# Spreading cumulative sums by DMA, one PSUM tile for two products, and modulation products in fours, in a two-layer hybrid trunk

## The chip, the cores and the metric

One core of one Trainium2 chip runs the whole program in one launch. Its engines are TensorE (PE in the rows, with PEld for its weight loads), VectorE (DVE), ScalarE (ACT), GpSimd (POOL) and SyncE (SP, which here only issues DMAs). The metric is the device time in microseconds, the median of the runs.

## What is computed

Two layers of a trunk run for a prompt (one sequence of 512 tokens) and eight samples (4 new tokens each, 1024 tokens of past), 544 tokens in all, with a model width of 1024. Per layer:

```python
mod = silu(c) @ w_ada + b_ada                   # shift, scale, gate, twice
h   = RMSNorm(x) * (1 + sc1) + sh1
P   = h @ w_in                                  # one projection for all mixers
A   = sparse GQA attention (indexer, top 256)
B   = causal pooling with windows 2, 4, 8, 16
C   = Mamba-2 SSD scan, gated, group-normed
x  += g1 * (sum_b sigmoid(G_b) * (branch_b @ w_branch_b)) @ w_out
x  += g2 * ((silu(g) * a) @ ffn_down),  [a, g] = causal_dwconv3(h2 @ ffn_up)
```

The change lies in C and in `mod`. C has 32 heads of width 64 in 4 groups with a state of 128, and works in chunks of 128 tokens:

```python
cs       = cumsum(dt * A)                       # per head, within a chunk
Lmat     = where(causal, exp(cs_l - cs_s), 0)
y_diag   = (C.B^T * Lmat) @ (x * dt)
states   = B^T @ (x * dt * exp(cs_end - cs))
prev     = scan over chunks of (prev * exp(cs_end) + states)
y        = y_diag + (C @ prev) * exp(cs) + D * x
```

The conditioning vectors `c` are 9 (one prompt, eight samples); `w_ada` has 1024 x 6144 entries per layer.

## The kernel before, in words

Tokens lie along the free dimension (a tile is 128 x 544), channels on the partitions. Each big product (`gemm`, L325) streams one 128 x 1024 weight tile from HBM through SP into one of four buffers `raw`; ACT rounds it to `wh`, DVE makes the remainder `wl` (three buffers each), and PE does three passes per 128-row piece and half of the tokens (L336). Results go to one of two PSUM tiles `psg`.

Small work is written as generators and put between the GEMMs: each `gemm` calls `pump` (L136), which advances every lane by its rate in steps, where a step ends at a `yield`. Lane "c" carries the SSD's generators with 4 steps per GEMM during `ssd` (L863), lane "a" the modulation with 1. The program order so written is not the final one: the framework orders each engine's instructions ahead of the run by their place in the program and by when it reckons their inputs and buffers to be ready, and then each engine follows that fixed order. Weight loads (`high_priority`, also those of `ada`) count as 300 places earlier. All tiles made by `self.t` share slots by tag; the tag of `seg`, `ecs`, `csT`, `prev`, `h0` and most others has 49 slots, each 128 x 544 fp32. PSUM has three kinds of tiles with two buffers each: `psg` for GEMMs, and `psa` and `psb` for the small work.

`ada` (L235) computes `mod` for a third of its 6144 columns. For each of 4 column blocks it loads 4 tiles `raw` of 512 KB (L250) and does two products per tile (L253): `sc` (32 columns, 9 in use) is the stationary operand, 512 columns stream, and the result lands on a group of 32 PSUM partitions. Eight products make two rounds over the four groups, and the second round accumulates. A `yield` stands after each tile. The first third of layer 0 runs at the very start, the other two in `pool_branch` and attention, and those of layer 1 during the FFN of layer 0.

`dt_chain` (L619 and on) computes the cumulative sums, once with tokens on the partitions (`cs`) and once with heads on the partitions (`csT`, L693 to L698, rounded and with the remainder in rows 32 to 63).

`ssd` goes over 4 groups. In each there are 6 GEMMs with convolution and SiLU (B, C and four x tiles), 4 GEMMs for z, and 8 half-length GEMMs of the group before (`branch`). Each x tile (two heads) has a `ssd_chain` (L956): transposes (L965), the products with `dt` on DVE (L968) and with the decay on POOL (L970); then per head a product on PE that spreads a row of `csT` over 128 partitions (L978, with a 0/1 column of `selc` as the stationary operand), four subtractions on DVE that read it from PSUM (L982), two exponentials on ACT (L984, L985) and the product with `cb` on POOL (L986); then the chunk states (L992), the scan `prev` on DVE (L998), eight products with 64 result columns into a PSUM tile `y` (L1006), `Y` on DVE (L1010), and three products with `prev` into a second PSUM tile `yo` (L1015), which DVE multiplies by `ecs` (L1017) and POOL adds to `Y` (L1018). There are 16 chains per layer and 6 yields in each.

`ssd_sample` (L1028) does the samples once per group. Eight small products spread the samples' part of `csT` (L1049). In two halves of four samples, four state tiles `h0` of 256 KB are loaded through SP (L1084), and after a `yield` four products (L1088) write four groups of 32 partitions of `psa`; then per sample one product (L1100), an update on POOL (L1103) and DVE (L1106), and a store through ACT's queue (L1107).

The wait of an engine's instruction holds all that stands behind it on the same engine, DMA issues on SP, ACT and POOL included.

Of the kernel before, what the change touches and what calls it, by code (L numbers as in the profile page):

```python
# [35 lines left out]
T = SEQ + NS  # L36
# [67 lines left out]
class Prog:  # L104
# [90 lines left out]
    def consts(self):  # L195
# [15 lines left out]
        self.selc = self.cp.tile([128, 32], F32R, name="selc")  # L211
        nc.vector.tensor_copy(self.selc, c[:, C_SEL:C_SEL + 32])
# [22 lines left out]
    def ada(self, l, s, first=False):  # L235
# [8 lines left out]
        for c in range(4):  # L244
            ps = self.P("ada1")
            for z in range(4):
                i = 4 * c + z
                with self.tc.high_priority(offset=WPRI):
                    raw = self.wr.tile([128, 1024], F32, name="raw", tag="raw")
                    nc.sync.dma_start(raw, a["w_ada"][l, s, i])  # L250
                for q in range(2):
                    k, g = 2 * z + q, 32 * (2 * (z % 2) + q)
                    nc.tensor.matmul(ps[g:g + 32, :], self.sc[:, k, :], raw[:, q * 512:(q + 1) * 512],  # L253
                                     start=(k < 4), stop=(k >= 4))
                if z < 3:
                    yield
# [362 lines left out]
    def dt_chain(self, kd):  # L619
# [73 lines left out]
        ct = self.csT = self.t("csT")  # L693
        cr = ct.bitcast(F32R)
        nc.vector.memset(ct[64:128, :], 0.0)
        for so, do in ((o[:32, :], slice(0, 512)), (o2[:32, :32], slice(512, T))):
            self.copy("dt_chain20", cr[:32, do], so)
            self.E("dt_chain19").tensor_tensor(cr[32:64, do], so, ct[:32, do], op=OP.subtract)  # L698
# [257 lines left out]
    def ssd_chain(self, q, jj, xs):  # L956
        nc, a, l = self.nc, self.a, self.l
        par = self.par[l][0]
        csr = self.csT.bitcast(F32R)
        g, bt, cb, Cc = q["g"], q["bt"], q["cb"], q["C"]  # L960
        j = 4 * g + jj
        self.E("ssd_chain1").tensor_copy(q["xss"][:, jj, :], xs[:, 512:])
# [10 lines left out]
        mts = []  # L973
        ecs = self.t("ecs")
        for e in range(2):
            hd = 2 * j + e
            ps = self.P("ssd_chain2")
            nc.tensor.matmul(ps, self.selc[:, hd:hd + 1].to_broadcast([128, 128]), csr[:, :512], start=True, stop=True)  # L978
            d = self.t("seg")
            for i in range(4):  # L980
                s_ = slice(i * 128, (i + 1) * 128)
                self.E("ssd_chain4").tensor_scalar(d[:, s_], ps[:, s_], self.cs[:, i, hd:hd + 1], 0.0,  # L982
                                        op0=OP.subtract, op1=OP.min)
            nc.scalar.activation(ecs[64 * e:64 * e + 64, 128:512], ps[64 * e:64 * e + 64, 128:], AF.Exp)  # L984
            nc.scalar.activation(d[:, :512], d[:, :512], AF.Exp)  # L985
            self.E("ssd_chain5").tensor_tensor(d[:, :512], d[:, :512], cb[:, :512], op=OP.mult)  # L986
            mts.append(d)
            yield
# [12 lines left out]
        nc.gpsimd.dma_start(a["o_ssdp"][l, j], prev[:, 384:512])  # L1001
        yield
        y = self.P("ssd_chain4")
        for i in range(4):
            for e in range(2):
                nc.tensor.matmul(y[64 * e:64 * e + 64, i * 128:(i + 1) * 128],  # L1006
                                 xdt[:, i * 128 + 64 * e:i * 128 + 64 * e + 64],
                                 mts[e][:, i * 128:(i + 1) * 128], start=True, stop=True)
# [3 lines left out]
        yield  # L1012
        yo = self.P("ssd_chain5")
        for i in range(1, 4):
            nc.tensor.matmul(yo[:, i * 128:(i + 1) * 128], prev[:, (i - 1) * 128:i * 128],  # L1015
                             Cc[:, i * 128:(i + 1) * 128], start=True, stop=True)
        self.E("ssd_chain8").tensor_tensor(ecs[:, 128:512], ecs[:, 128:512], yo[:, 128:], op=OP.mult)  # L1017
        self.E("ssd_chain9").tensor_tensor(Y[:, 128:512], Y[:, 128:512], ecs[:, 128:512], op=OP.add)  # L1018
# [9 lines left out]
    def ssd_sample(self, q):  # L1028
        nc, a, l, c = self.nc, self.a, self.l, self.c
        par = self.par[l][0]  # L1030
        csr = self.csT.bitcast(F32R)
        g, cb, Cc, xss = q["g"], q["cb"], q["C"], q["xss"]
        ps = self.P("ssd_sample1")
# [13 lines left out]
        ps = self.P("ssd_sample2")  # L1047
        for i in range(8):
            nc.tensor.matmul(ps[:, i * 32:(i + 1) * 32], self.selc[:, 8 * g + i:8 * g + i + 1].to_broadcast([128, 128]),  # L1049
                             csr[:, 512:], start=True, stop=True)  # L1050
        ecs, mt = self.t("secs"), self.t("smt")
        for e in range(2):
            nc.scalar.activation(ecs[64 * e:64 * e + 64, :128].rearrange("p (j t) -> p j t", j=4),
                                 ps[64 * e:64 * e + 64, :256].rearrange("p (j e t) -> p e j t", e=2, t=32)[:, e],
                                 AF.Exp)
        m3 = mt[:32, :256].rearrange("p (h t) -> p h t", h=8)
        self.E("ssd_sample4").tensor_tensor(m3, ps[:32, :256].rearrange("p (h t) -> p h t", h=8),
# [17 lines left out]
        for hf in range(2):  # L1075
# [6 lines left out]
            h0s = [self.t("h0") for z in range(4)]  # L1082
            for z in range(4):
                nc.sync.dma_start(h0s[z][:, :512], a["h0"][l, g, 4 * hf + z])  # L1084
            yield
            for z in range(4):
                b = 4 * hf + z
                nc.tensor.matmul(qp[32 * z:32 * z + 32, :], cm[:, 32 * b:32 * b + 32], h0s[z][:, :512],  # L1088
# [680 lines left out]
```

## Time and profile before

| what | value |
|---|---|
| runs shown | 3218.22, 3217.64, 3216.38 us; median 3217.64 |
| profiled execution | 3219.4 us, span 3217.6 us, mean granted clock 0.985 |
| PE | 3117.6 us busy (97%), 24322 instructions |
| DVE | 2229.4 us (69%), 4827 |
| ACT | 1258.1 us (39%), 2228 |
| POOL | 892.9 us (28%), 1271 |
| DMA | 376.85 MB, mean 117 GB/s |

The span goes from the first to the last instruction. Busy time counts the time in which at least one instruction of an engine is under way; matmuls are pipelined, so several overlap. The two SSD stages lie at about 130 to 620 us (layer 0) and 1760 to 2260 us (layer 1). An fp32 product counts as two matmul instructions; those of L336, L978, L1049 and L1100 have rounded operands (fp32r) and count as one.

### The profile page before, as it was taken

What the parts mean: (1) busy time and instruction counts of PE and PEld (TensorE: products, weight loads), DVE (VectorE), ACT (ScalarE), POOL (GpSimd) and SP (SyncE); (2) the same over time, 40 slices, a digit from 0 to 9 for tenths busy, and PEclk for the clock granted to TensorE, in tenths of its full rate; (3) what the DMA queues carried; (4) which work ended last, traced back from release to release, by engine and by line L of the source; (5) the groups of instructions that cost most, each with busy time, mean ns of one, the idle gap of its engine ahead of it and who ended that gap; (6) DMA issues with size and microseconds to landing.
All of it is one profiled execution on the core that took longest, in us unless ns stands there. A gap on an engine that the chain in (4) does not pass through costs nothing. (4 is left out here: it accounts for less than half of the span.)

```text
span 3217.6 us, 63012 instructions
## 1 busy us (share of the span) xinstructions
PE 3117.6 (97%) x24322; PEld 2834.3 (88%) x24322; DVE 2229.4 (69%) x4827; ACT 1258.1 (39%) x2228; POOL 892.9 (28%) x1271
## 2 busy tenths in 40 slices
PE   7999999999999999999999999999999999999999
PEld 5987898999896788888989978989999967899999
DVE  5687788679878655444566877886799976564554
ACT  4344443333236534333443444433342365352432
POOL 2373445421021002111223544455120210030211
PEclk8999999999999999999999999999999999999999
DMA  6332332345433434445334323233233234333322
GB/s 231 104 104 77 110 95 101 105 151 179 164 117 129 157 133 115 147 146 147 105 104 122 98 82 106 89 96 119 95 129 117 91 125 154 106 84 94 78 98 78
DMA packets 303102, 376.85 MB, mean 117 GB/s; under 512 B 177362, under 2 KB 186930, under 8 KB 302802
## 3 DMA queue, kind: packets, MB, share of 16 engines
q1 hardware_dynamic: 116514, 315.94, 29.3%
q10 hardware_dynamic: 181216, 42.05, 6.4%
q0 software_dynamic: 5072, 14.83, 1.2%
q8 instruction: 192, 3.15, 0.4%
q14 instruction: 108, 0.88, 0.1%
HBM read 330.34 MB, written 33.79 MB: 113 GB/s over the span
## 5 line engine op out<-in xcount | busy, mean ns | idle before, releaser
L177 ACT ACTIVATE wh<-raw 128x1024 fp32r<-128x1024 f32 (+2 forms) x434 | 424.9, 980 | 1199.7 <-PE psg L336 909.6
L336 PE MATMUL psg<-hh,wh 128*128 128x272 f32 x4064 | 863.7, 292 | 7.8 <-ACT cacc L839 5.4
L336 PE MATMUL psg<-hl,wh 128*128 128x272 f32 x4064 | 856.0, 290 | 0.0
L336 PE MATMUL psg<-hh,wl 128*128 128x272 f32 x4064 | 853.6, 290 | 0.0
L322 DVE TENSOR_TENSOR wl<-raw,wh 128x1024 fp32r<-128x1024 f32 (+2 forms) x434 | 510.5, 1176 | 354.1 <-ACT wh L177 349.8
L336 PEld LDWEIGHTS psg<-hh,wh 128*128 128x128 f32 x4064 | 642.6, 189 | 61.9 <-issue 28.1
L336 PEld LDWEIGHTS psg<-hh,wl 128*128 128x128 f32 x4064 | 643.9, 189 | 17.1 <-issue 15.3
L336 PEld LDWEIGHTS psg<-hl,wh 128*128 128x128 f32 x4064 | 644.1, 189 | 15.9 <-issue 14.4
L841 POOL COPY sti<-cu 128x32 f32<-128x32 f32 x136 | 91.3, 672 | 588.9 <-ACT cu L177 588.6
L846 DVE SCALAR_TENSOR_TENSOR cacc<-cu,half,cacc 128x511 f32<-128x511 f32 x144 | 134.9, 937 | 6.8 <-ACT cacc L839 6.3
L336 PE MATMUL psg<-fh,wh 128*128 128x272 f32 x648 | 135.4, 291 | 2.6 <-DVE resid L460 2.6
L855 ACT ACTIVATE th<-cacc 128x544 f32<-128x544 f32 x92 | 60.5, 657 | 196.1 <-DVE cacc L849 187.5
L454 DVE SCALAR_TENSOR_TENSOR x<-psg,mod,x 128x272 f32<-128x272 f32 x64 | 32.0, 500 | 151.6 <-PE psg L336 142.6
L336 PE MATMUL psg<-fl,wh 128*128 128x272 f32 x648 | 133.7, 287 | 0.0
L336 PE MATMUL psg<-fh,wl 128*128 128x272 f32 x648 | 133.7, 288 | 0.0
L336 PEld LDWEIGHTS psg<-fh,wh 128*128 128x128 f32 x648 | 101.2, 188 | 14.3 <-issue 6.7
L336 PE MATMUL psg<-oh,wh 128*128 128x272 f32 x512 | 110.4, 294 | 0.0
L336 PE MATMUL psg<-ol,wh 128*128 128x272 f32 x512 | 109.5, 291 | 0.0
L336 PE MATMUL psg<-oh,wl 128*128 128x272 f32 x512 | 109.0, 292 | 0.0
L856 DVE SCALAR_TENSOR_TENSOR cacc<-th,cacc 128x544 f32<-128x544 f32 x92 | 71.3, 775 | 49.2 <-ACT th L855 49.0
L986 POOL TENSOR_TENSOR seg<-seg,cb 128x512 f32<-128x512 f32 x64 | 88.9, 1392 | 54.3 <-ACT seg L985 46.8
L336 PEld LDWEIGHTS psg<-fl,wh 128*128 128x128 f32 x648 | 101.7, 188 | 0.0
(469 smaller groups left out, 6232.4 us busy)
## 6 DMA issues: line engine op xcount, KB each, us to landing
raw<-wk SPq DMA_DIRECT2D x326, 512.0 KB, 3.5
raw<-w_ada SPq DMA_DIRECT2D x96, 512.0 KB, 3.5
h<-h SPq DMA_DIRECT2D x64, 256.0 KB, 3.8
raw<-wk SPq DMA_DIRECT2D x64, 256.0 KB, 2.8
o_ssds<-hn ACTq DMA_DIRECT2D x64, 256.0 KB, 2.2
raw<-wd SPq DMA_DIRECT2D x32, 448.0 KB, 3.4
kvr<-ckv SPq DMA_DIRECT2D x48, 256.0 KB, 3.6
kvw<-ckv SPq DMA_DIRECT2D x48, 256.0 KB, 4.0
```

What stands on the lines that cost most here:

```text
L177: self.nc.scalar.activation(out, src, AF.Copy)
L322: self.last_wl = self.E("weights1").tensor_tensor(wl[:, :n], raw[:, :n], wh[:, :n].bitcast(F32), op=OP.subtract).ins
L336: nc.tensor.matmul(o[:, c, :HC], w[:, k * 128:(k + 1) * 128], x[:, c * HC:(c + 1) * HC], start=(k == 0 and first), stop=(k == K - 1 and last))
L454: self.E("resid1").scalar_tensor_tensor(x[:, :HC], o[:, 0, :HC], g[:, 0:1], x[:, :HC], op0=OP.mult, op1=OP.add)
L841: self.E("conv1").tensor_copy(st[:, i, :, W - 1:], new)
L846: self.E("conv3").scalar_tensor_tensor(acc[:, s:512], u[:, :512 - s], wc, acc[:, s:512], op0=OP.mult, op1=OP.add)
L855: nc.scalar.activation(th, acc, AF.Tanh)
L856: self.E("silu21").scalar_tensor_tensor(acc, th, 1.0, acc, op0=OP.add, op1=OP.mult)
L986: self.E("ssd_chain5").tensor_tensor(d[:, :512], d[:, :512], cb[:, :512], op=OP.mult)
```

## The change

It has three parts. The cumulative sums with heads on the partitions are stored to DRAM once per layer (`csp`, `css`) and spread over the partitions by DMAs from ACT's queue: one row per head into a tile `seg` at the head of the chain, one row per group for the samples into `csb`. The chain's order changes: the states come ahead of the exponentials, the sums' exponential now has 128 partitions and multiplies C instead of the product with `prev`, and the products with `prev` (64 result columns each, two per chunk) add to the same PSUM tile as the diagonal ones; `yo`, `ssd_chain9` and three of the six yields go. In `ssd_sample` the `h0` loads of the first half stand at the head and those of the second right behind the first half's products, with one yield less per half. In `ada` two tiles are loaded before four products are issued; the number of yields stays.

```diff
-        self.selc = self.cp.tile([128, 32], F32R, name="selc")
-        nc.vector.tensor_copy(self.selc, c[:, C_SEL:C_SEL + 32])
...
@@ ada
-            for z in range(4):
-                i = 4 * c + z
-                with self.tc.high_priority(offset=WPRI):
-                    raw = self.wr.tile([128, 1024], F32, name="raw", tag="raw")
-                    nc.sync.dma_start(raw, a["w_ada"][l, s, i])
-                for q in range(2):
-                    k, g = 2 * z + q, 32 * (2 * (z % 2) + q)
-                    nc.tensor.matmul(ps[g:g + 32, :], self.sc[:, k, :], raw[:, q * 512:(q + 1) * 512],
-                                     start=(k < 4), stop=(k >= 4))
-                if z < 3:
+            for pair in range(2):
+                raws = []
+                for z in (2 * pair, 2 * pair + 1):
+                    with self.tc.high_priority(offset=WPRI):
+                        raw = self.wr.tile([128, 1024], F32, name="raw", tag="raw")
+                        nc.sync.dma_start(raw, a["w_ada"][l, s, 4 * c + z])
+                    raws.append(raw)
+                    if z % 2 == 0:
+                        yield
+
+                for k4 in range(4):
+                    nc.tensor.matmul(ps[32 * k4:32 * k4 + 32, :], self.sc[:, 4 * pair + k4, :],
+                                     raws[k4 // 2][:, (k4 % 2) * 512:(k4 % 2) * 512 + 512],
+                                     start=(pair == 0), stop=(pair == 1))
+                if pair == 0:
                     yield
@@ dt_chain
-        ct = self.csT = self.t("csT")
-        cr = ct.bitcast(F32R)
-        nc.vector.memset(ct[64:128, :], 0.0)
-        for so, do in ((o[:32, :], slice(0, 512)), (o2[:32, :32], slice(512, T))):
-            self.copy("dt_chain20", cr[:32, do], so)
-            self.E("dt_chain19").tensor_tensor(cr[32:64, do], so, ct[:32, do], op=OP.subtract)
+        ct = self.t("csT")
+        self.copy("dt_chain20", ct[:32, :512], o[:32, :])
+        self.copy("dt_chain20", ct[:32, 512:], o2[:32, :32])
+
+        self.csp = self.dp.tile([32, 512], F32, name="csp%d" % l)
+        self.css = self.dp.tile([4, 256], F32, name="css%d" % l)
+        nc.scalar.dma_start(self.csp, ct[:32, :512])
+        nc.scalar.dma_start(self.css.rearrange("g (h t) -> (g h) t", h=8), ct[:32, 512:])
@@ ssd_chain
+        segs = [self.t("seg") for e in range(2)]
+        for e in range(2):
+            nc.scalar.dma_start(segs[e][:, :512], self.csp[2 * j + e:2 * j + e + 1, :].to_broadcast([128, 512]))
...
-        mts = []
-        ecs = self.t("ecs")
-        for e in range(2):
-            hd = 2 * j + e
-            ps = self.P("ssd_chain2")
-            nc.tensor.matmul(ps, self.selc[:, hd:hd + 1].to_broadcast([128, 128]), csr[:, :512], start=True, stop=True)
-            d = self.t("seg")
-            for i in range(4):
-                s_ = slice(i * 128, (i + 1) * 128)
-                self.E("ssd_chain4").tensor_scalar(d[:, s_], ps[:, s_], self.cs[:, i, hd:hd + 1], 0.0,
-                                        op0=OP.subtract, op1=OP.min)
-            nc.scalar.activation(ecs[64 * e:64 * e + 64, 128:512], ps[64 * e:64 * e + 64, 128:], AF.Exp)
-            nc.scalar.activation(d[:, :512], d[:, :512], AF.Exp)
-            self.E("ssd_chain5").tensor_tensor(d[:, :512], d[:, :512], cb[:, :512], op=OP.mult)
-            mts.append(d)
-            yield
...
+        cds = []
+        for e in range(2):
+            hd = 2 * j + e
+            d, cd = segs[e], self.t("ecs")
+            nc.scalar.activation(cd[:, 128:512], d[:, 128:512], AF.Exp)
+            for i in range(4):
+                s_ = slice(i * 128, (i + 1) * 128)
+                self.E("ssd_chain4").tensor_scalar(d[:, s_], d[:, s_], self.cs[:, i, hd:hd + 1], 0.0,
+                                        op0=OP.subtract, op1=OP.min)
+            nc.scalar.activation(d[:, :512], d[:, :512], AF.Exp)
+            self.E("ssd_chain5").tensor_tensor(d[:, :512], d[:, :512], cb[:, :512], op=OP.mult)
+            self.E("ssd_chain8").tensor_tensor(cd[:, 128:512], cd[:, 128:512], Cc[:, 128:512], op=OP.mult)
+            cds.append(cd)
         yield
         y = self.P("ssd_chain4")
         for i in range(4):
+            s_ = slice(i * 128, (i + 1) * 128)
             for e in range(2):
-                nc.tensor.matmul(y[64 * e:64 * e + 64, i * 128:(i + 1) * 128],
-                                 xdt[:, i * 128 + 64 * e:i * 128 + 64 * e + 64],
-                                 mts[e][:, i * 128:(i + 1) * 128], start=True, stop=True)
+                nc.tensor.matmul(y[64 * e:64 * e + 64, s_], xdt[:, i * 128 + 64 * e:i * 128 + 64 * e + 64],
+                                 segs[e][:, s_], start=True, stop=(i == 0))
+            for e in range(2 if i else 0):
+                nc.tensor.matmul(y[64 * e:64 * e + 64, s_], prev[:, (i - 1) * 128 + 64 * e:(i - 1) * 128 + 64 * e + 64],
+                                 cds[e][:, s_], start=False, stop=True)
...
-        yo = self.P("ssd_chain5")
-        for i in range(1, 4):
-            nc.tensor.matmul(yo[:, i * 128:(i + 1) * 128], prev[:, (i - 1) * 128:i * 128],
-                             Cc[:, i * 128:(i + 1) * 128], start=True, stop=True)
-        self.E("ssd_chain8").tensor_tensor(ecs[:, 128:512], ecs[:, 128:512], yo[:, 128:], op=OP.mult)
-        self.E("ssd_chain9").tensor_tensor(Y[:, 128:512], Y[:, 128:512], ecs[:, 128:512], op=OP.add)
-        yield
@@ ssd_sample
+        def states(hf):
+            h0s = [self.t("h0") for z in range(4)]
+            for z in range(4):
+                nc.sync.dma_start(h0s[z][:, :512], a["h0"][l, g, 4 * hf + z])
+            return h0s
+        nxt = states(0)
+        csb = self.t("csb")
+        nc.scalar.dma_start(csb[:, :256], self.css[g:g + 1, :].to_broadcast([128, 256]))
...
-        ps = self.P("ssd_sample2")
-        for i in range(8):
-            nc.tensor.matmul(ps[:, i * 32:(i + 1) * 32], self.selc[:, 8 * g + i:8 * g + i + 1].to_broadcast([128, 128]),
-                             csr[:, 512:], start=True, stop=True)
...
-            h0s = [self.t("h0") for z in range(4)]
-            for z in range(4):
-                nc.sync.dma_start(h0s[z][:, :512], a["h0"][l, g, 4 * hf + z])
-            yield
+            h0s = nxt
             for z in range(4):
                 b = 4 * hf + z
                 nc.tensor.matmul(qp[32 * z:32 * z + 32, :], cm[:, 32 * b:32 * b + 32], h0s[z][:, :512],
                                  start=(hf == 0), stop=(hf == 1))
-            if hf:
+            if not hf:
+                nxt = states(1)
+            else:
```

In `ssd_sample` the two readers of the spread samples' sums (L1053 and L1057) read `csb` from SBUF instead of PSUM.

## Rows read from the trace of the kernel before

**Rows 1.** The page, part 4: the chain that ended last, by engine.
```profile
PE 33%; DVE 3%; issue 1%; DMA 1%; POOL 1%; ACT 1%; ACTq 0%; SPq 0%; DVEq 0%; POOLq 0%
```

**Rows 2.** Stages: from:to, length, busy PE PEld DVE ACT POOL, clock, DMA share, GB/s.
```profile
0.00:50.00 50.00, 32.00 (x156) 16.64 (x156) 25.57 (x84) 22.33 (x49) 11.82 (x39) 0.90 0.85 297
...
130.00:620.00 490.00, 477.65 (x3652) 430.12 (x3651) 381.24 (x718) 200.60 (x344) 248.33 (x284) 0.99 0.31 98
1760.00:2260.00 500.00, 488.16 (x3696) 436.88 (x3695) 385.95 (x722) 203.18 (x348) 251.16 (x284) 0.98 0.31 98
```

**Rows 3.** Timeline of PE near 1242 us: start us, us, instruction.
```profile
1241.64 0.42 PE L336 MATMUL psg<-hl,wh 128*128 128x272 f32 x2
1241.89 0.41 PE L336 MATMUL psg<-hh,wl 128*128 128x272 f32 x2
1242.23 1.05 PE L253 MATMUL psb<-raw,sc 128*32 128x512 f32 x4
1243.21 0.52 PE L336 MATMUL psg<-hh,wh 128*128 128x272 f32 x2
```

**Rows 4.** Timeline of PE near 718 us.
```profile
717.77 1.07 PE L253 MATMUL psb<-raw,sc 128*32 128x512 f32 x8
718.77 0.52 PE L1213 MATMUL psg<-ph,wh 128*128 128x272 f32 x2
```

**Rows 5.** Timeline of PE near 421 us and 200 us.
```profile
420.83 0.40 PE L978 MATMUL psa<-csT,selc 128*128 128x512 f32 x1
421.06 0.29 PE L336 MATMUL psg<-ol,wh 128*128 128x272 f32 x1
...
199.98 0.96 PE L1049 MATMUL psa<-csT,selc 128*128 128x32 f32 x8
200.79 0.49 PE L336 MATMUL psg<-hh,wl 128*128 128x272 f32 x2
```

**Rows 6.** Timeline of PE near 430 us.
```profile
428.26 0.43 PE L1006 MATMUL psb<-seg,xdt 128*64 128x128 f32 x2
428.63 0.39 PE L336 MATMUL psg<-oh,wl 128*128 128x272 f32 x1
...
431.12 1.09 PE L1006 MATMUL psb<-seg,xdt 128*64 128x128 f32 x14
432.14 0.94 PE L1015 MATMUL psb<-cacc,prev 128*128 128x128 f32 x6
432.83 0.50 PE L336 MATMUL psg<-oh,wh 128*128 128x272 f32 x2
```

**Rows 7.** Timeline of PE near 227 us.
```profile
226.31 1.04 PE L1088 MATMUL psa<-h,cm 128*32 128x512 f32 x2
227.29 0.52 PE L336 MATMUL psg<-hh,wh 128*128 128x272 f32 x2
```

**Rows 8.** DVE groups by shape: count, busy us, mean ns, idle before.
```profile
L982 DVE TENSOR_SCALAR seg<-psa,dtc 128x128 f32<-128x128 f32 x256 | 71.3, 341 | 11.4 <-PE psa L978 11.3
L1017 DVE TENSOR_TENSOR ecs<-ecs,psb 128x384 f32<-128x384 f32 x32 | 17.4, 545 | 2.2 <-PE psb L1015 2.2
L1381 DVE TENSOR_SCALAR S<-S,asm 128x128 f32<-128x128 f32 x32 | 8.7, 284 | 0.7
```

**Rows 9.** DVE groups by shape: L849, SSD (half) and FFN (fhalf).
```profile
L849 DVE SCALAR_TENSOR_TENSOR cacc<-sti,half,cacc 128x32 f32<-128x32 f32 x144 | 79.5, 552 | 3.0 <-POOL sti L841 2.2
L849 DVE SCALAR_TENSOR_TENSOR cacc<-sti,fhalf,cacc 128x32 f32<-128x32 f32 x88 | 21.3, 241 | 0.0
```

**Rows 10.** Timeline near 168 us: POOL, then DVE.
```profile
167.00 1.73 POOL L986 TENSOR_TENSOR seg<-seg,cb 128x512 f32<-128x512 f32 x1
...
167.51 1.28 DVE L849 SCALAR_TENSOR_TENSOR cacc<-sti,half,cacc 128x32 f32<-128x32 f32 x1
```

**Rows 11.** DMA issues (us to landing), and the issue itself (ns min/median/max).
```profile
h<-h SPq DMA_DIRECT2D x64, 256.0 KB, 3.8
...
L1107 ACTq DMA_DIRECT2D o_ssds<-hn x64: 338/339/555, 224.6 to 2259.0; - x64
```

More of the change, by code (lines that the diff above doesn't have):

```diff
@@ L958, in ssd_chain @@
         par = self.par[l][0]
-        csr = self.csT.bitcast(F32R)
         g, bt, cb, Cc = q["g"], q["bt"], q["cb"], q["C"]
         j = 4 * g + jj
+        segs = [self.t("seg") for e in range(2)]
+        for e in range(2):
+            nc.scalar.dma_start(segs[e][:, :512], self.csp[2 * j + e:2 * j + e + 1, :].to_broadcast([128, 512]))
         self.E("ssd_chain1").tensor_copy(q["xss"][:, jj, :], xs[:, 512:])
@@ L1030, in ssd_sample @@
         par = self.par[l][0]
-        csr = self.csT.bitcast(F32R)
         g, cb, Cc, xss = q["g"], q["cb"], q["C"], q["xss"]
+        def states(hf):
[6 more added lines that the diff above has]
+        nc.scalar.dma_start(csb[:, :256], self.css[g:g + 1, :].to_broadcast([128, 256]))
         ps = self.P("ssd_sample1")
@@ L1053, in ssd_sample @@
             nc.scalar.activation(ecs[64 * e:64 * e + 64, :128].rearrange("p (j t) -> p j t", j=4),
-                                 ps[64 * e:64 * e + 64, :256].rearrange("p (j e t) -> p e j t", e=2, t=32)[:, e],
+                                 csb[64 * e:64 * e + 64, :256].rearrange("p (j e t) -> p e j t", e=2, t=32)[:, e],
                                  AF.Exp)
         m3 = mt[:32, :256].rearrange("p (h t) -> p h t", h=8)
-        self.E("ssd_sample4").tensor_tensor(m3, ps[:32, :256].rearrange("p (h t) -> p h t", h=8),
+        self.E("ssd_sample4").tensor_tensor(m3, csb[:32, :256].rearrange("p (h t) -> p h t", h=8),
                                 self.cs[:32, 4, hs, None].to_broadcast([32, 8, 32]), op=OP.subtract)
```

## The prediction

> **What bounds the kernel now.** I read the page first: TensorE (PE) is busy 97% of the span, as the table above has it, and of the chain that ended last it holds 33 of the 40 points given [rows 1]. So I asked next how full each stage is. In the two SSD stages PE stands idle only 490.0 - 477.7 = 12.3 us and 11.8 us [rows 2]; VectorE (DVE) comes second with 77 to 78%, ScalarE (ACT) has 41%, GpSimd (POOL) 50%. The first 50 us are another case: DMA is 85% busy at 297 GB/s and DMA sets the pace [rows 2]. Elsewhere a microsecond of PE time that goes away is a microsecond of span, as long as DVE, ACT and POOL keep up. A busy sum does not give that time, since matmuls overlap; I take it from the timeline of PE, from the start of one piece to the start of the next. "Visit" means a run of instructions of one line between two pieces of the big GEMM (L336). These prices are at the full clock (granted 0.99 and 0.98 in the SSD stages [rows 2]).
>
> **A. Modulation products in fours (L253).** Each fp32 product is two instructions. A visit of two products (four instructions) lasts from 1242.23 to 1243.21, 0.98 us; two GEMM instructions take 1241.89 - 1241.64 = 0.25 us, so without the visit the next would have started at 1242.14, and entering costs 0.09 more: 1.07 us [rows 3]. A visit of eight instructions, where two pairs happened to meet, lasts 1.00 us, 1.09 with the entry [rows 4]: products that write different groups of 32 partitions run at the same time, four as cheaply as two. After the first 52 us there are 71 visits: 61 of four instructions, 7 of eight, three odd ones. The 61 become 30.5 of eight: 61 x 1.07 - 30.5 x 1.09 = 32 us, and the odd ones (20 instructions) give some 2 more: **34 us**. The 64 instructions of the first 50 us I set at nothing, because DMA hides them [rows 2]; holding two of the four weight buffers until a quad runs can cost some 3 us there. Later the weight stream keeps two buffers of four: at 297 GB/s [rows 2] a 512 KB tile takes some 2 us, and a GEMM of 48 instructions at 0.125 takes 6 us [rows 3].
>
> **B. The spreading products go.** A selection product (L978, 128x512) holds PE for 421.06 - 420.83 = 0.23 us, and there are 64: 14.7 us. Eight small ones of a group's samples (L1049) hold it 0.81 us, eight times: 6.5 us [rows 5]. Together **21 us**. The two PSUM tiles that they took are no longer asked for.
>
> **C. One PSUM tile per chain.** Now 28 of 32 chains send two instructions of L1006 alone (0.37 us), then fourteen (1.02 us), then six of L1015 (0.69 us) [rows 6]. After, six full-width instructions become twelve of half width. At 1.02/14 = 0.073 us they cost 0.87, or 0.18 more; one change of shape between the two lines, and its drain, goes. I take **0**. Bounds: 6 us lost (0.18 x 32) and 14 us won if the lone first pair is no longer sent ahead (0.37 + 0.09 each).
>
> **D. State loads earlier (L1084, L1088).** The four products of half a group also write four groups of 32 partitions, but 30 of their 40 visits hold one product only, and a visit of one costs as much as a visit of four: 226.31 to 227.29 is 0.98 us [rows 7], against 1.00 for eight instructions [rows 4]. With entries: 30 x 1.07 + 6 x 1.08 + 4 x 1.09 = 43 us, and 16 full visits would be 17. So up to 26 us lie here. The loads take 3.8 us to land [rows 11]; the change issues the first half's four pumped steps earlier and the second half's before the four updates instead of right ahead of the products. They need free slots of the shared pool of 49, which the longer lives of `seg`, `ecs` and `h0` make scarcer (only `csT` leaves). On SP they stand among the weight loads, which run two GEMMs ahead; a load that waits for a slot holds the weights behind it, covered for some 12 us. I take **14**, about half, because slots are scarce; bounds 0 and 26.
>
> **E. What is added.** ACT issues 64 loads of `seg`, 8 of `csb` and 4 stores, 76 DMAs. A 128-partition DMA holds ACT's queue 0.34 us [rows 11]: 26 us more on an engine at 41%. Behind each stand the copies of weights and of GEMM results; what is copied there is buffered two GEMMs deep, so a third of a microsecond is hidden; with no cover it would be the 26 us. The exponentials stay as many and as long in columns, so I count them as before. How long a row spread over 128 partitions takes to land no row shows: a 256 KB load needs 3.8 us [rows 11], and I take that, with anything from a third to three times of it as bounds, all of it behind the cover. The load starts at the head of a chain, and transposes, `xdd`, states and `prev` cover it; without that cover it would be 3.8 us for each of 32 chains. The subtraction waits anew for the first exponential, which reads the same tile; behind it on DVE stand weight remainders (L322), two GEMMs ahead of PE.
> The other addition is DVE's. The subtraction (L982) reads PSUM now, 256 x 0.341 us; a DVE operation of its size from SBUF (L1381) takes 0.284. The product on L1017 (0.545 us, one PSUM operand) is done twice per chain, both operands in SBUF [rows 8]. Against that stands what SBUF operands suffer beside POOL: the 128x32 step on L849 takes 0.241 us in the FFN, but 0.552 on average in the SSD stages [rows 9]. The timeline shows why: one that started at 167.51 ended at 168.79, just after POOL's multiply, which ended at 168.73 [rows 10]. With that mean wait of 0.31, DVE gets 256 x (0.284 + 0.31 - 0.341) = 65 and 64 x (0.545 + 0.31) - 32 x 0.545 = 37, some **102 us** more on 767 in 990, so 91% of a stage shortened to some 955. It stays below PE, but later results of DVE will stall it oftener. No row has that price. I bound it by 20 us of gain (today's 24 us of idle PE nearly gone, since fewer PSUM tiles are asked for) and 48 of loss (twice today's idling more), and take **12 us of new stalls**, half of today's idling again, because DVE stays below PE.
> [...]
>
> **The sum.** 34 + 21 + 0 + 14 - 12 = 57 us. The profiled execution took 3219.4 us with a span of 3217.6; the median of the runs, 3217.64, lies 1.8 below it. I take the 57 off the median: **3161 us**. A measurement tells about 0.2% here, 6.4 us.
>
> **The rivals.**
> *Everything fits (0.13):* all sixteen visits of D whole, no lone first pair, no new stall: 34 + 21 + 14 + 26 = 95, so 3123. For it: eight-instruction visits occur already. Against it: slots.
> *Late engines eat half (0.16):* ACT's issues and DVE's waits stall PE some 40 us: 3189. For it: DVE's 91%.
> *The quads come apart (0.08):* the second raw tile of a pair is late, the order sends two products ahead, and A gives nothing: 3195. Against it: weight loads are far ahead and 7 visits of eight formed by chance.
> *DVE becomes the bound (0.09), slower:* the place is the four subtractions and two products per head in the SSD stages, the price a wait w for POOL on each of 320 operations. DVE is then busy 767 + 3 + 320w. It decides once this passes 990 plus the 34 that A gives, at w = 0.79 us; the waiting operation of rows 10 waited 1.28 - 0.24 = 1.04. At w = 0.9 the stages take 1058, 68 more than now, less A: 3252. Against it: 0.31 is what L849 sees on average, and POOL loses the addition on L1018. [...]
> *The removed products were slack (0.02):* only if others hold the stages already, about 3217; rows 2 speak against it.
> The forecast keeps 0.52.
>
> **Range and chances.** 3115 to 3205 takes in the forecast with its bounds, most of the best case, the late engines and the split quads; the slower case stays out. Faster: 0.52 + 0.13 + 0.08 and nearly all of 0.16, 0.87. Within 0.2%: 0.04. Slower: 0.09.
>
> **What would show it.** A: visits of L253 with eight instructions, about 40 after the start, of 1.0 us. B: no selection products, no gaps in their place. C: one PSUM tile and a line with 28 instructions per chain. D: visits of the state products with eight instructions. E: the subtraction near 0.6 us on average with a long tail, DVE near 90% in the SSD stages and PE's idle time there some 35 us in all. I am wrong if DVE there passes 97%, if PE waits for `seg` or its loads, if quads stand as pairs, or if weight copies on ACT come late behind a DMA that waits for a slot.

## The result and the profile after

The changed kernel takes **3245.88 us** (median of 5 runs, 3240.77 to 3251.70) beside 3218.22 for the kernel before: ratio **1.0079**, 95% interval 1.0059 to 1.0099. It is slower by 0.8%, where I had forecast 3161 and a gain; it lies above the whole of my range. The profiled execution took 3240.77 us with a span of 3239.0 us and a mean granted clock of 0.971 (0.985 before).

The chain that ended last, part 4 of the page of the kernel after (answers to [rows 1]):

```profile
PE 29%; DVE 2%; issue 1%; ACT 1%; DMA 1%; POOL 0%; SPq 0%; ACTq 0%; POOLq 0%
```

No other engine has taken PE's place as the bound. The stages of the kernel after, columns as in [rows 2]:

```profile
130.00:620.00 490.00, 443.01 (x3470) 407.65 (x3469) 367.64 (x700) 187.84 (x324) 194.84 (x242) 0.94 0.34 108
1760.00:2260.00 500.00, 452.42 (x3554) 418.36 (x3554) 373.96 (x716) 193.92 (x334) 195.47 (x240) 0.95 0.34 107
```

PE stands idle 47.0 + 47.6 = 94.6 us there, 24.2 before, and its clock falls from 0.99 and 0.98 to 0.94 and 0.95. DVE, which I had feared, is at 75%, less than before. So PE waits, and nobody else is full: that is the picture of a **latency**, not of a busy engine. For what does it wait? The waits of PE in the kernel after, 130 to 620 us (engine, tile, line, releaser: us in total, times, longest):

```profile
PE psg L339 <- ACT cacc L844: 15.4, 2, 8.0
PE psb L1012 <- POOL seg L1004: 13.0, 6, 4.1
PE psb L1104 <- DVE hn L1110: 7.1, 3, 2.8
```

Before, the longest three of this list were 2.9, 2.6 and 1.4 us. The first two lines gave me two theories.

**Order.** PE's result products (L1012) wait for the masks that POOL finishes (L1004). The timeline of the kernel after, all engines, one chain of the second group (start us, us, instruction; in brackets the idle time of the engine before it and what ended it):

```profile
318.81 0.69 DVE L975 TENSOR_TENSOR xdt<-psa,dtc 128x512 f32<-128x512 f32 x1 [4.36 <-PE psb L1012]
...
319.58 1.05 POOL L977 TENSOR_TENSOR xdd<-xdt,dtc 128x512 f32<-128x512 f32 x1 [3.75 <-DVE xdt L975]
...
321.91 1.05 PE L983 MATMUL psb<-xdd,bt 128*128 128x128 f32 x8
...
323.00 0.28 ACT L177 ACTIVATE prev<-psb 128x128 f32<-128x128 f32 x1 [0.26 <-PE psb L983]
323.17 0.93 ACT L998 ACTIVATE ecs<-seg 128x384 f32<-128x384 f32 x2
...
323.93 0.47 DVE L989 SCALAR_TENSOR_TENSOR prev<-prev,dac,psb 128x64 f32<-128x64 f32 x2
...
324.31 0.68 DVE L1001 TENSOR_SCALAR seg<-seg,dtc 128x128 f32<-128x128 f32 x3
...
325.08 0.63 ACT L1003 ACTIVATE seg<-seg 128x512 f32<-128x512 f32 x1 [0.98 <-DVE seg L1001]
...
325.79 1.45 POOL L1004 TENSOR_TENSOR seg<-seg,cb 128x512 f32<-128x512 f32 x1 [5.16 <-ACT seg L1003]
...
327.30 0.47 PE L1012 MATMUL psb<-seg,xdt 128*64 128x128 f32 x1 [4.08 <-POOL seg L1004]
```

Read down the starts: `xdt`, `xdd`, the states on PE, and only then ACT's copy of the states, the exponentials, the subtractions, POOL's product, and PE again, 8.5 us after `xdt`, one link after another (two of the eight subtractions, at 320.07, had found a place earlier). Between the end of the states at 322.96 and 327.30 PE has only the rest of a GEMM, and stands idle 4.08 us.

**Queue.** The other line is the copy of a GEMM result on ACT. The timeline of ACT in the kernel after, with its queue:

```profile
206.03 7.18 ACTq L889 DMA_DIRECT2D sti<-st_conv  x4
213.25 1.30 ACTq L1041 DMA_DIRECT2D csb<-css  x1
214.60 0.81 ACT L844 ACTIVATE cacc<-psg,half 128x544 f32<-128x544 f32 x1 [8.83 <-DMA sti<-st_conv]
```

Small loads, which were there before, and the new `csb` load stand ahead of the copy for 8.8 us; four such places cost PE 31 us (8.0, 7.4, 9.5 and 6.5).

### The profile page after: what moved, and what is told of

Same layout as the page of the kernel before. It is cut to its first block, busy times and chain, and to the rows that moved or that the text cites. A ratio compares the mean times of both kernels' runs of the same rounds, so it can differ in the third digit from the quotient of the medians.

```text
span 3239.0 us, 63177 instructions
## 1 busy us (share of the span) xinstructions
PE 3062.8 (95%) x24386; PEld 2830.2 (87%) x24386; DVE 2236.2 (69%) x4852; ACT 1259.5 (39%) x2228; POOL 828.3 (26%) x1239
## 5 line engine op out<-in xcount | busy, mean ns | idle before, releaser
L846 POOL COPY sti<-cu 128x32 f32<-128x32 f32 x136 | 79.5, 584 | 555.5 <-ACT cu L177 555.5
L851 DVE SCALAR_TENSOR_TENSOR cacc<-cu,half,cacc 128x511 f32<-128x511 f32 x144 | 127.4, 885 | 16.9 <-ACT cacc L844 16.2
L1004 POOL TENSOR_TENSOR seg<-seg,cb 128x512 f32<-128x512 f32 x64 | 88.9, 1390 | 144.5 <-ACT seg L1003 144.3
L1001 DVE TENSOR_SCALAR seg<-seg,dtc 128x128 f32<-128x128 f32 x256 | 105.0, 447 | 13.1 <-DMA seg<-csp 12.8
L1578 POOL TENSOR_TENSOR cacc<-cacc 128x544 f32<-128x544 f32 x44 | 62.3, 1415 | 161.0 <-DVE cacc L861 161.0
```

The costliest lines, as they stand in the source:

```text
L846: self.E("conv1").tensor_copy(st[:, i, :, W - 1:], new)
L851: self.E("conv3").scalar_tensor_tensor(acc[:, s:512], u[:, :512 - s], wc, acc[:, s:512], op0=OP.mult, op1=OP.add)
L1001: self.E("ssd_chain4").tensor_scalar(d[:, s_], d[:, s_], self.cs[:, i, hd:hd + 1], 0.0, op0=OP.subtract, op1=OP.min)
L1578: self.E("ffn3").tensor_tensor(s_, s_, aa, op=OP.mult)
```

## The experiments

All times are medians beside runs of the kernel before on the same chip, with the 95% interval of the ratio. I name kernels by their labels. The runs come in sets, and the kernel before itself differs by up to 4 us from set to set (3218.12 to 3222.32), so a difference between kernels of two sets carries that much more doubt.

**1. One part alone: quads (e1), earlier state loads (e4).** e1 is the kernel before with only the `ada` part of the diff, e4 with only this (the first line at the head of `ssd_sample`):

```diff
+        nxt = states(0)
...
-            h0s = [self.t("h0") for z in range(4)]
-            for z in range(4):
-                nc.sync.dma_start(h0s[z][:, :512], a["h0"][l, g, 4 * hf + z])
-            yield
+            h0s = nxt
...
+            if not hf:
+                nxt = states(1)
```

> Before, with the modulation products in fours and nothing else. My prediction priced this part at 34 us, which would be 3184. The stages of the changed kernel in which these products run were 9 and 16 us shorter, so the theory that the SSD part alone makes the change slow expects about 25 us: 3190 to 3196, ratio 0.992. If the quads are what hurts elsewhere (a weight buffer held for longer), the gain is under 10 us.

> Before, with the state loads issued earlier and nothing else. My prediction priced this at 14 us of gain, bounds 0 and 26, so 3204 (3192 to 3218), seen as visits of the four state products in one piece. If the slots of the shared pool are the limit, the loads wait there, hold the weights behind them on SP, and the time rises by 5 us or more.

Measured: e1 3189.58, ratio 0.9906 (0.9891 to 0.9920), 30 us faster; e4 3210.11, ratio 0.9968 (0.9959 to 0.9978), 10 us faster. Both parts gain, so the loss is in the rest. In e4 the state products come in 20 visits instead of 40; its timeline of PE shows one that is whole and one that is not:

```profile
215.25 1.04 PE L1092 MATMUL psa<-h,cm 128*32 128x512 f32 x2
...
219.22 1.07 PE L1092 MATMUL psa<-h,cm 128*32 128x512 f32 x8
220.22 0.52 PE L336 MATMUL psg<-hh,wl 128*128 128x272 f32 x2
```

**2. The loads taken off ACT (e3).** The changed kernel with

```diff
-                nc.scalar.dma_start(st[:, i, :, 0:3], a["st_conv"][l, g, i])
+                nc.sync.dma_start(st[:, i, :, 0:3], a["st_conv"][l, g, i])
...
-        nc.scalar.dma_start(csb[:, :256], self.css[g:g + 1, :].to_broadcast([128, 256]))
+        nc.sync.dma_start(csb[:, :256], self.css[g:g + 1, :].to_broadcast([128, 256]))
```

> The changed kernel with the six small loads of a group's conv state and the spread of a group's sample sums issued from SP instead of ScalarE; the 64 spreads of the chains stay on ScalarE. Queue theory: the four waits of PE for the copy of a GEMM result, 31 us together, go: 3215 to 3222, ratio 0.992. Order theory: the waits for the masked matrix stay and the gain is under 10 us. If SP then holds the weights behind a load that waits for a slot, PE waits for weight loads, which the trace would show, and the time rises.

Measured: 3241.37, ratio 1.0067 (1.0054 to 1.0080): 4 us better than the change, and the intervals overlap. The waits of PE in e3, 130 to 620 us, tell why:

```profile
PE psb L1012 <- POOL seg L1004: 13.2, 6, 3.9
PE psb L750 <- ACT rel L748: 8.6, 2, 6.9
PE psg L339 <- ACT cacc L844: 6.4, 2, 4.7
```

The wait for the copy shrank from 15.4 to 6.4, and a wait for a relu, a little later on the same engine, grew from 3.1 to 8.6; PE's idle time in the two stages is 92.6 us instead of 94.6. **The queue theory falls as the main cause.** The largest single wait in a list need not be what the time hangs on: as these rows read, PE had no other work at that spot, so the next late engine held it instead.

**3. The steps of a chain restored (e2), and both edits (e6).** e2 is the changed kernel with three yields put back, nothing else:

```diff
         nc.gpsimd.dma_start(a["o_ssdp"][l, j], prev[:, 384:512])
+        yield
...
             cds.append(cd)
-        yield
+            yield
...
                                        op0=OP.mult, op1=OP.add)
+        yield
         yield
```

With four steps per GEMM, three steps put a whole chain between two GEMMs; with six, the result products fall behind the next one.

> The changed kernel with the steps of a chain cut as they were (six steps for each chain instead of three, so that the states and the result products fall into different GEMMs again); no operation is added or removed. Order theory (the chain's exponentials, subtractions and POOL multiply lie bare because states and result products now stand between the same two GEMMs): PE's waits for the masked matrix, some 27 us in the two SSD stages, mostly go, and the time falls by 20 to 35 us, to 3210 to 3225. Queue theory (DMA issues on ScalarE stand ahead of the copies of GEMM results): the 31 us of waits for that copy stay, and the time falls by less than 10. Theory of VectorE's waits for GpSimd: no change within 5 us.

> The changed kernel with both edits: the steps of a chain cut as before, and the small loads of a group issued from SP. With the chain's steps back (3212) PE still waited four times, 28.6 us in all, for the copy of a GEMM result behind these loads on ScalarE. Queue theory: those waits go now that the order gives other work, 3185 to 3192. If the stall only turns into the next one, as it did when the loads were moved alone (a wait for the result of a relu, then the conv chain): above 3203.

Measured: e2 3211.77, ratio 0.9971 (0.9958 to 0.9984), 34 us off; e6 3203.10, ratio 0.9948 (0.9929 to 0.9968), some 8 more, with intervals that overlap. The waits of PE in e2, 130 to 620 us:

```profile
PE psg L339 <- ACT cacc L844: 14.0, 2, 8.0
PE psb L1013 <- POOL seg L1005: 6.1, 5, 2.5
```

The wait for the masks is down from 13.0 to 6.1 us, and the one for the copy is nearly as it was. So the order of the work counts, but e2 is still some 30 us above what quads and earlier loads alone would make, though it has no selection products any more.

**4. The remaining parts one by one (e5, e7, e8).** e5 is quads and earlier loads. e7 adds to it the single PSUM tile alone: PE still spreads `csT`, `ecs` gets 128 partitions per head and is multiplied by C, both products go into `y`. e8 adds to e5 the spreading by DMA alone, with two PSUM tiles. In both the masks stay ahead of the states, with six steps. The core of e8:

```diff
-            ps = self.P("ssd_chain2")
-            nc.tensor.matmul(ps, self.selc[:, hd:hd + 1].to_broadcast([128, 128]), csr[:, :512], start=True, stop=True)
-            d = self.t("seg")
+            d = segs[e]
+            nc.scalar.activation(ecs[64 * e:64 * e + 64, 128:512], d[64 * e:64 * e + 64, 128:512], AF.Exp)
...
```

> Before, with the quads (alone 30 us faster) and the earlier state loads (alone 10 us faster), nothing else. If the two add: 3180, ratio 0.987. If the loads of the quads' second weight buffer and the earlier state loads hold each other up on SP: nearer to 3190.

> Quads and earlier state loads (some 3180), and of the rest only the one PSUM tile: both products of a chain add into it, the decay is multiplied onto the second operand for each head on VectorE (one product more for each chain), while TensorE still spreads the cumulative sums, and the chain keeps six steps in the old order. My prediction set this part at 0 (bounds 6 lost, 14 won): 3166 to 3186. If the single tile is what hurts (nothing of the second product can run until the result products of the first have their masks, and the product on VectorE comes ahead of PE's line): 3195 or more.

> Quads and earlier state loads (some 3180), and of the rest only the spreading by DMA: the selection products go, ScalarE issues the loads of each chain and group, the subtraction reads SBUF; the chain keeps its six steps in the old order and its two products stand apart in two PSUM tiles. If the spreading itself is sound, as my prediction had it (21 us off, at most 12 of stalls): 3160 to 3172. If the DMA issues on ScalarE, the landing of the loads, or the subtraction beside GpSimd is what loses time whatever the order: 3185 or more, with waits of PE for a copy on ScalarE or for the masked matrix.

Measured: e5 3183.10 (0.9888, 0.9870 to 0.9905); e7 3173.46 (0.9850, 0.9832 to 0.9869), 10 less than e5; e8 3153.48 (0.9784, 0.9764 to 0.9804), 30 less than e5 and below the 3160 to 3172 I expected. With the old order each of the four parts pays. What is left as a suspect is the new order.

**5. Order, crossed with the number of steps (e9, e10), and the loads again (e11).** e9 is the whole change with the block of exponentials, subtractions and mask products put back ahead of the states, in six steps; e10 the same in three; e11 is e9 with the edit of e3.

```diff
+        cds = []
+        for e in range(2):
...
         stp = self.P("ssd_chain3")
...
         nc.gpsimd.dma_start(a["o_ssdp"][l, j], prev[:, 384:512])
-
-        cds = []
-        for e in range(2):
...
         yield
         y = self.P("ssd_chain4")
```

> The whole change, but the chain in the old order: spread, subtraction, exponentials and mask product ahead of the states, and six steps for each chain. The parts alone gave: quads and earlier loads 3183, with the single PSUM tile 10 less, with the DMA spreading 30 less. Order theory: only the order loses, so the parts add to 3183 - 10 - 30 = 3143, 3138 to 3152. If single tile and DMA spreading hurt each other (the products on VectorE now both from SBUF, beside GpSimd): 3165 or more.

> The whole change with the exponentials ahead of the states again, but the chain still in three steps, so that masks, states and result products fall between the same two GEMMs. The six steps with the exponentials behind gave 34 us. If number of steps and place cost independently: some 34 above the six-step kernel of this set, about 3177. If the place alone does the harm: within 10 us of that kernel. If the steps do most of it: above 3190.

> The whole change in the old order with six steps, and the small loads of a group (conv state, sample sums) issued from SP. If the loads on ScalarE still hold copies of GEMM results there: 5 to 15 us under the kernel without this edit. If the old order covers them, as it covered them before the change: within 5 us of it.

Measured (ratio, us):

| masks | six steps | three steps |
|---|---|---|
| ahead of the states | e9 3142.94, 0.9761 (0.9746 to 0.9775) | e10 3164.02, 0.9817 (0.9797 to 0.9838) |
| behind the states | e2 3211.77, 0.9971 (0.9958 to 0.9984) | the change 3245.88, 1.0079 (1.0059 to 1.0099) |

As times the parts add to within 1 us (3143 forecast); by the ratios it is some 5 us, since the two sets' kernels before differ by 4. The place costs 3211.77 - 3142.94 = 69 us with six steps, the steps 21 us with the masks ahead and 3245.88 - 3211.77 = 34 with the masks behind, both together 103. So place and steps don't cost independently: e10 lies between the two cases I had named for it (3177, and within 10 us of e9). e9 is also the version that **beats both kernels**, by 79 us against before. e11 takes 3149.90 (0.9781, 0.9764 to 0.9797), 7 us more than e9 with overlapping intervals: with the old order nothing is gained by taking the small loads off ACT. That PE's other work covers the burst there, as before the change, fits this and the waits below.

The stages and the waits of PE in e9, 130 to 620 us (columns of the stages as in [rows 2]):

```profile
130.00:620.00 490.00, 473.74 (x3836) 436.48 (x3835) 405.68 (x776) 206.35 (x356) 229.66 (x271) 0.99 0.39 120
1760.00:2260.00 500.00, 483.41 (x3880) 448.60 (x3880) 408.24 (x786) 202.55 (x354) 219.08 (x261) 0.98 0.39 119
```

```profile
PE psa L972 <- DVE cb L958: 6.0, 1, 6.0
PE psb L1105 <- DVE hn L1111: 4.4, 3, 1.7
PE psb L1012 <- POOL seg L990: 2.3, 2, 1.9
```

Idle time of PE is 16.3 + 16.6 = 32.9 us, the clock is back at 0.99 and 0.98, the wait for the masks is down from 13.0 to 2.3, and that for the copy from 15.4 to 1.4, though nothing was done about it. In e10, where only the steps are missing, the wait for the masks is back:

```profile
PE psb L1011 <- POOL seg L990: 9.2, 6, 6.0
```

**6. The order alone, in the kernel before (e12).** Before, with the selection products, subtractions, exponentials and mask products moved as a block behind the states, six steps, nothing added.

> Before, with one thing moved: in each chain the spreading, the subtraction, the exponentials and the mask product stand behind the states, as in the changed kernel; six steps, two products apart, spreading by TensorE, nothing added or removed. Order theory: the place alone loses time, 20 to 60 us, so 3238 to 3280, with waits of PE for the masked matrix. If the place hurts only together with the DMA spreading or the single tile: within 6 us of before.

Measured: 3298.90, ratio 1.0245 (1.0229 to 1.0261): 77 us slower, more than the 20 to 60 expected. The place needs neither the DMAs nor the single tile to do its harm. The stages of e12:

```profile
130.00:620.00 490.00, 455.09 (x3372) 408.80 (x3371) 353.86 (x680) 190.22 (x324) 213.63 (x251) 0.95 0.29 89
1760.00:2260.00 500.00, 464.27 (x3461) 418.77 (x3462) 361.39 (x691) 190.71 (x322) 216.32 (x258) 0.96 0.31 92
```

One of my signs failed, though: PE's waits put down to the masks are only 1.6 us in either stage there, and the copies of GEMM results (13 us in each) lead the list. A list of waits names where a lateness comes out, which need not be where it starts.

**7. What in the place does it (e13, e14).** e13 is e2 with the states' matmuls left ahead, but their evacuation moved behind the mask products:

```diff
-        prev = self.t("prev")
-        self.copy("ssd_chain10", prev[:, :128], stp[:, :128])
...
-        nc.gpsimd.dma_start(a["o_ssdp"][l, j], prev[:, 384:512])
         yield
...
             cds.append(cd)
-            yield
+            if e == 0:
+                yield
+        prev = self.t("prev")
+        self.copy("ssd_chain10", prev[:, :128], stp[:, :128])
...
+        nc.gpsimd.dma_start(a["o_ssdp"][l, j], prev[:, 384:512])
+        yield
```

e14 is e2 with the copy of the first state on DVE (`CPD` gets `ssd_chain10`).

> The whole change with six steps and the states' matmuls ahead of the masks, as changed, but the evacuation of the states (the copy on ScalarE, the six steps of the scan on VectorE, the store) moved behind the mask products. The kernel with evacuation ahead took 3212, the one with everything in the old order 3143. Queue theory of the place (the copy and the scan wait for the states' product, and the exponentials and subtractions stand behind them on the same two engines, though their own loads have landed): 3143 to 3160, and the time from the states' product to the second mask falls from 6.9 to some 3.6 us. If the place of the matmuls on TensorE is what counts: 3200 or more.

> The kernel with six steps and the masks behind the states (3212), with only the copy of the first state moved from ScalarE to VectorE. If ScalarE's queue is what holds the exponentials (it waited 31 us in each SSD stage for the states in this kernel): 3175 to 3195. If the scan on VectorE ahead of the subtractions does it alone or as well: within 10 us of 3212.

Measured: e13 **3153.01**, ratio 0.9791 (0.9775 to 0.9807), 59 of the 69 us regained; e14 3207.98, ratio 0.9959 (0.9946 to 0.9973), within 4 us of e2. The tile `prev` in the kernel after, 130 to 620 us (the engine that works on it sat idle before it, us and times, until):

```profile
  PE psb L983: 33.9, 12
  ACT prev L177: 15.1, 6
```

and in e13:

```profile
  DVE prev L1006: 22.4, 12
  PE psb L983: 5.5, 5
```

ACT's copy waited 33.9 us for the states and DVE's scan 15.1 us for that copy, with the exponentials and the subtractions behind them in the same two queues, although their loads had landed: a load of `seg` takes 3.6 us in the median, and DVE waited 12.8 us for one in the whole program, 15 times in 256 subtractions. With the evacuation behind the masks, the wait for the states is 5.5 us (8.1 in e9, 5.8 before); the 22.4 are POOL's wait ahead of the store, which is 24.5 in e9 and so not what costs. From the trace, the time from the end of the states' last product to the end of the second mask product is, in the median of 32 chains:

| evacuation ahead of the masks | us | masks ahead of it | us |
|---|---|---|---|
| the change | 6.9 | before | 3.0 |
| e2 | 6.9 | e9 | 3.6 |
| e14 | 6.9 | e10 | 3.8 |
| e12 | 6.5 | e13 | 3.9 |

Some 3.3 us more per chain, times 32, is 106 us of latency, of which 69 come out. The number of steps leaves this latency as it is (e2 beside the change, e10 beside e9); what it alters is how long PE has to wait for the masks. e14 shows that it isn't ACT alone: with the copy on DVE the latency is still 6.9, so the scan is as much in the way of the subtractions. The 10 us between e13 and e9, and which of the three yields matters, the runs do not separate.

## Why the prediction was wrong

**Where the time went.** Parts: quads 30, earlier loads 10 (7 together with the quads: 3189.58 - 3183.10), one tile 10, spreading 30, all together 79 us off (e9). Order: 103 us on, 69 for the place and 34 for the steps that went. 103 - 79 = 24, against 27.7 measured; the 4 between them are what the two sets' kernels before differ by.

**A. Right.** I said 34, alone it gave 30 (26 to 35 by the interval). The visits of eight look as I priced them; the timeline of PE in the kernel after:

```profile
729.95 1.07 PE L255 MATMUL psb<-raw,sc 128*32 128x512 f32 x8
730.94 0.52 PE L1217 MATMUL psg<-ph,wh 128*128 128x272 f32 x2
```

0.99 us, against 1.00 in [rows 4]. Of 45 visits after the first 52 us, 34 are of eight instructions; five of four are left.

**B. Right in sign, too small by 9.** I said 21; with its DMAs, and no new stall, the spreading gives 30 (e8 against e5). PE's idle time in the two stages is 31.7 us in e5 and 31.8 in e8, so the 12 us of new stalls that I charged in E were not there. That is 9 more than the products as I priced them. In the kernel before all 128 take 29.9 us from start to next start, where mine took 21.2, so the 9 may well be time around the products; no run shows it apart.

**C. Mis-sized.** I said 0 with bounds 6 and 14; 10 us came (e7 against e5; e9 against e8 gives 7 by the ratios and 11 by the times). The reason is not the one behind my upper bound: 26 lone visits of two instructions are still there in e7. What the 10 us are, the runs do not separate; nor does any run show apart the drain at a change of shape that I set against 0.18 us a chain.

**D. Nearly right.** 14 said, 10 measured alone, with 20 visits instead of my 40 before and 16 at best.

**E. This step failed.** I priced what was added and took the rest of the chain as it stood: "The exponentials stay as many and as long in columns, so I count them as before", and "transposes, `xdd`, states and `prev` cover" the load. Both sentences are true, and they miss what the move does. The document ahead of the prediction says that the states come ahead of the exponentials and that three of six yields go; I gave neither a term. What I treated as cover for the load had become **a chain of waits ahead of everything after it**: states on PE, copy on ACT, scan on DVE, and behind them in these queues the exponentials and subtractions that need none of it. The three yields that went took away the GEMM that used to lie between masks and result products: PE's wait for the masks in 130 to 620 us is 13.0 without them and 6.1 with them (e2).

Its other prices: ACT's issues took 0.33 us at the least, 0.35 in the median and up to 1.69 (my 0.34), and their landing 3.6 (my 3.8). For DVE's 102 us the rows of the kernel after, groups by shape as in [rows 8, 9]:

```profile
L1001 DVE TENSOR_SCALAR seg<-seg,dtc 128x128 f32<-128x128 f32 x256 | 105.0, 447 | 13.1 <-DMA seg<-csp 12.8
L1005 DVE TENSOR_TENSOR ecs<-ecs,cacc 128x384 f32<-128x384 f32 x64 | 35.2, 550 | 0.0
L854 DVE SCALAR_TENSOR_TENSOR cacc<-sti,half,cacc 128x32 f32<-128x32 f32 x144 | 63.1, 438 | 2.2 <-DMA sti<-st_conv 1.7
```

105.0 - 71.3 + 35.2 - 17.4 = 51.5 us more, half of what I charged: the subtraction waits 447 - 283 = 164 ns on average (its mean less its median) and not 310, the product not at all, and the old wait on L849 (552 ns, now L854) has become shorter.

**The rivals.** None had the mechanism. "Late engines eat half" said that ACT and DVE would hold PE, by 40 us, but put it down to DMA issues and to waits for POOL. e8 has all 76 DMAs and the subtraction from SBUF, and PE's idle time in the two stages is 31.8 us there, beside 31.7 in e5; e9, with the new products on DVE as well, has 32.9. "DVE becomes the bound" had the sign, not the cause: DVE fell to 75%. The slower side had 0.09, all of it on that one mechanism.

**The clock** makes the loss larger than the idle time. Over the whole program PE is idle 3239.0 - 3062.8 = 176.2 us in the kernel after and 3136.7 - 3032.0 = 104.7 in e9, 71.5 less, while the span falls by 102.3. The other 31 us are PE being busy longer with the same 24386 instructions, at a mean granted clock of 0.971 against 0.983. e12 beside the kernel before shows the same: 53 us more of idle time, 25 more of busy time. A stretch of the kernel after with two waits of some 4 us in it, columns as in [rows 2]:

```profile
300.00:335.00 35.00, 21.74 (x186) 18.40 (x186) 22.43 (x53) 10.88 (x23) 10.61 (x11) 0.80 0.24 79
```

The result products of 312 to 333 us and of the whole program (count, ns min/median/max, first and last start):

```profile
L1012 PE MATMUL psb<-seg,xdt x32: 417/421/474, 313.3 to 331.8; 128*64 128x128 f32 x32
```

```profile
L1012 PE MATMUL psb<-seg,xdt x512: 272/273/476, 157.4 to 2267.4; 128*64 128x128 f32 x171
```

In that stretch, at a granted clock of 0.80, a product takes 421 ns in the median instead of the 273 of the whole program. So the 71.5 us more of idle time came with 31 us of slower work; I had priced stalls at their length alone. The granted clock is 0.80 where PE is busy 21.74 of 35 us, 0.94 over the stage, where it is busy 443.01 of 490, and 0.99 in e9 with 473.74 of 490. The runs show that the two go together, not what lowers the clock.

## What to carry to other kernels

When a change moves a block within a program, cost the move as a term of its own: write down, engine by engine, what now stands ahead of the block in each engine's queue and for what that waits, also where no operation is added. Where a generator's yields decide between which GEMMs its products fall, count them before and after; a yield that goes can take the cover of a whole chain with it. And before repairing the longest wait in a list, ask whether PE would have other work at that spot; if it would not, the next late engine can take its place, as in e3 (15.4 us down to 6.4, and 3.1 up to 8.6).

## What the runs showed of the hardware

In the kernel after DVE and POOL hold each other up, in both directions. The subtraction in place (one SBUF input, L1001) takes 265 ns at the least, 283 in the median and 1425 at the most. 48 of its 256 take over 350 ns; each of them runs beside an operation of POOL (27 of them beside its mask product, 1.30 us in the median) and ends 0.08 to 0.09 us behind that operation's end. The product with two SBUF inputs (L1005) never takes over 558 ns in the kernel after; in the five places where the two start within 0.25 us of each other, it is POOL's product that is the longer one, with 1.46 to 1.75 us. POOL and DVE near 462 and 446 us:

```profile
462.47 1.55 POOL L1004 TENSOR_TENSOR seg<-seg,cb 128x512 f32<-128x512 f32 x1 [6.05 <-ACT seg L1003]
...
445.79 3.16 POOL L1004 TENSOR_TENSOR seg<-seg,cb 128x512 f32<-128x512 f32 x2 [4.01 <-ACT seg L1003]
```

```profile
462.31 0.56 DVE L1005 TENSOR_TENSOR ecs<-ecs,cacc 128x384 f32<-128x384 f32 x1
...
445.83 0.55 DVE L1005 TENSOR_TENSOR ecs<-ecs,cacc 128x384 f32<-128x384 f32 x1
```

The mask product that meets DVE's product takes 1.55 us near 462 and 1.75 near 446 (the first of the two there), of 1.30 in the median. Near 462 us and in two more places DVE's product starts 0.17 to 0.24 us before POOL's, and POOL takes 1.46 to 1.55. Near 446 us and in one more place POOL's record starts 0.04 us before DVE's, and still POOL is the one that is stretched, to 1.75. In all five POOL ends 1.15 us after DVE's product does. I had charged this wait to DVE alone.

A burst of small DMA issues on ACT can hold its queue far longer than such issues mostly take: four issues of 12 KB loads took 7.18 us (206.03 us in the kernel after), where an issue of such a load takes 0.55 us at the least and 0.68 in the median of 48. The burst was there before the change too: in the kernel before four of these issues took 5.04 us at 198.28.
